# A block of a streaming encoder: the gated product of up pair 19 and the sums over it are issued one weight chunk later

## The chip, the cores and the metric

The kernel runs on one core of one Trainium2 chip. The metric is the time of one execution on the device, in microseconds (us). The kernel before takes 693.18 us (median of 3 runs, 693.14 to 693.18).

The core has a matrix engine (PE, with its weight loads shown apart as PEld), a vector engine (DVE), a scalar engine (ACT), a general engine (POOL) and one that only starts transfers (SP). Each works through its own instructions in the order in which they were issued, and waits for the others through semaphores.

## The reference

One residual layer over x of 512 positions by 1024 channels, in float32:

```
h = rms_norm(x)
proj = h @ w_in                      # 1024 -> conv B, C, in | q, k, v | forget logits | gates
y_conv = (cb * conv3(cc * cin)) @ w_out_conv
y_attn = forgetting_attention(q, k, v, log_f) @ w_out_attn
x = x + (g_conv * y_conv + g_attn * y_attn) @ w_o
h = rms_norm(x)
up = causal_dwconv(h @ w_up, conv_ffn_w)      # 1024 -> 2 * 2816, then 3 taps over the positions
a, b = split(up)
x = x + (silu(a) * b) @ w_down                # 2816 -> 1024
return rms_norm(x)
```

The change lies in the last part: the product with w_up, the taps, silu(a) * b, and the preparation of that product for w_down.

## The kernel before

**Float32 out of two parts.** Every product is made of three passes of the matrix engine, over a high and a low part of each operand. A chunk of weights (128 partitions by 1024 columns for w_up) is loaded into a `raw` tile by SP, `split` lets ACT copy it into the high part (`wh_...`, L275) and DVE subtract that from it to get the low part (`wl_...`, L279). There are two buffers for each of the two parts, so the parts of a chunk can be written once the matrix engine is through with the chunk two places ahead. The chunks come in one fixed stream: for the channel mixer `up0`, `up1`, ... `up43`, with some places taken by chunks `P` and `F` (below).

**The channel mixer.** The 2816 hidden channels are 22 blocks of 128. Pair j is the block j of a and the block j of b, thus the chunks up(2j) and up(2j+1). A pair's product goes through `up`: 8 blocks of 128 rows times 3 passes times 2 halves of 256 positions are 48 matmuls into one PSUM bank for each chunk. `block` puts the passes of the first two row blocks in another order: 8 matmuls with the high part of the weights, 4 with the low part (L327), and then 36 in the plain order (L309). The result is scaled into `fz` (L1170, DVE), goes through the three taps into `fu` (one ACT instruction, L566, and two of DVE, L567 and L570), and `glu` takes silu of a (ACT, L1231) and multiplies by b.

Pairs are taken two at a time (number q = j // 2): the even pair's product is `ge{q}` (POOL, L1234), the odd one's `go{q}` (L1241, on POOL for pairs 17 and 19). From both come sums (`t13`, `t24`: L1251 to L1256, DVE) that serve a product with seven instead of eight block products, and the high and low parts of those sums: `gh` (ACT, L1260) and `gl` (DVE, L1261), which are called the forms here. The forms of one q are four instructions on ACT and four on DVE. The matrix engine reads them only in the phase that follows (`dn`, the product with w_down, with the chunks P and F). The tile of `go{q}` and its sums has one buffer, so go9 may be written only when the forms of go8 are made.

There are two such phases. Phase 0 has pairs 0 to 11, phase 1 has pairs 12 to 21. Pairs 14 and 17 (`SUP[1]`) also take the way with seven products; their results are put together by `merge`, which fills a list with work tagged `e`.

**What sets the order.** Work that isn't urgent is put on a list `later`, as (chunk number from which it is due, a price, tags, function). `split` ends with `run_later`, which takes from the front of the list what is due, as far as a budget of 1.7 us for a chunk reaches, and issues it with the condition that it comes behind the high and the low part of the chunk just split (`after_split`). `flush_only` issues all of a tag at once, also behind the chunk split last. Ahead of the product of q, `glu` flushes all forms of the earlier q.

**POOL and the transfers.** The weights F are sums of weights, made in DRAM while the kernel runs: SP copies (L208), POOL issues additions by transfer (L211, `f34` to `f41` for phase 1), in six steps that `slot()` issues one after the other, once for each chunk. These instructions stand in POOL's row between the products.

The functions below hold the changed lines and what calls them. (go8 belongs to pairs 16 and 17, go9 to pairs 18 and 19; the chunk behind which `sums` comes is up40, the first of pair 20.)

Of the kernel before, what the change touches and what calls it, by code (L numbers as in the profile page):

```python
# [8 lines left out]
F32 = mybir.dt.float32  # L9
F32R = mybir.dt.float32r  # L10
AF = mybir.ActivationFunctionType
ALU = mybir.AluOpType

P = 128
# [4 lines left out]
H = 8  # L19
# [3 lines left out]
NP = FFN // P  # L23
# [19 lines left out]
PHASES = ((0, 12), (12, NP))  # L43
NG = 42
NF = 7
# [15 lines left out]
SUP = ((1, 2, 5), (14, 17))  # L61
# [9 lines left out]
def block_kernel(ctx, tc, xT, vecs, wv, win, wmix, wo, wup, wst, wdp, outT):  # L71
# [3 lines left out]
    nc = tc.nc  # L75
# [6 lines left out]
    def keep(ins):  # L82
        return tc.keep_in_program_order(ins)
# [25 lines left out]
    tbl = cp.tile([4 * H, 1], F32, tag="tbl", name="tbl")  # L109
# [17 lines left out]
    n = 0  # L127
# [28 lines left out]
    later = []  # L156
    held = dict.fromkeys(NRAW, 0)

    def after_split():

        st = ExitStack()
        for ins in order.values():
            st.enter_context(tc.issue_after(ins))
        return st
# [53 lines left out]
    def slot():  # L218

        while todo_bg and todo_bg[0][0] <= make_forms.slot:  # L220
            todo_bg.pop(0)[1]()
        make_forms.slot += 1
# [24 lines left out]
    def flush_only(tags):  # L247

        while n := [n for n, w in enumerate(later) if set(w[2]) & set(tags)]:
            with after_split():  # L250
                later.pop(n[0])[3]()
# [84 lines left out]
    eps = ex[:, NT : NT + 1]  # L336
# [52 lines left out]
    at = ExitStack()  # L389
# [62 lines left out]
    for kb in range(KB):  # L452
        x = xs[kb]
# [12 lines left out]
        for cs in cuts:  # L466
            keep(nc.vector.scalar_tensor_tensor(
                xgl[:, kb, cs], x[:, cs], col(G1 + kb), xgh.bitcast(F32)[:, kb, cs],
                op0=ALU.mult, op1=ALU.subtract,
# [94 lines left out]
    def taps(u, z, w):  # L564

        nc.scalar.activation(u, z, AF.Copy, scale=col(w + 2))  # L566
        nc.vector.scalar_tensor_tensor(  # L567
            u[:, 1:], z[:, : S - 1], col(w + 1), u[:, 1:], op0=ALU.mult, op1=ALU.add
        )
        nc.vector.scalar_tensor_tensor(  # L570
            u[:, 2:], z[:, : S - 2], col(w), u[:, 2:], op0=ALU.mult, op1=ALU.add
        )
# [111 lines left out]
    for t in range(NT):  # L684
        src = pa[t][:, 4 * HD : VW].unsqueeze(1).to_broadcast([P, 4, H])
        nc.vector.tensor_scalar_mul(zn[:, t], src, rc1[:, t : t + 1])

    n = 4 * H
    bf, me, mo = vec[:n, BF : BF + 1], vec[:n, ME : ME + 1], vec[:n, MO : MO + 1]
    z, e, o = (ap.tile([n, S], F32, tag="pp", name=nm, bufs=NPP) for nm in ("fz", "fe", "fo"))  # L690
# [69 lines left out]
    def x_sums(qs):  # L760
        b11, b12, b21, b22 = (xq[:, qs, i, :] for i in range(4))

        def f():
            nc.vector.tensor_sub(b11, b11, b12)
            nc.vector.tensor_sub(b12, b22, b12)

        def g():
            nc.vector.scalar_tensor_tensor(b22, b11, -1.0, b22, op0=ALU.mult, op1=ALU.subtract)
            nc.vector.scalar_tensor_tensor(b21, b22, -1.0, b21, op0=ALU.mult, op1=ALU.subtract)

        return f, g

    k = len(parts) + 2
    for q in (0, 2):
        f, g = x_sums(slice(q, q + 2))
# [8 lines left out]
    for idx in late:  # L784
        kind, i = divmod(idx, 4)
# [7 lines left out]
    n = len(units)  # L793
    make_forms(0, len(GATES), "gate")
    for i in range(n + LA):
# [8 lines left out]
        if 0 <= i - LA < n:  # L804
            pr, e, qb = units[i - LA]
# [5 lines left out]
    halves_of = "p (h c) -> p h c"  # L811
# [6 lines left out]
    def split_next():  # L818
        if len(parts) == chunk.n and stream[chunk.n][0] not in ("dp1", "dp2"):
            split()  # L820
# [85 lines left out]
    k = [c[0] for c in stream].index("mix0")  # L906
# [52 lines left out]
    for j in range(KB):  # L959
        gs = []  # L960
# [25 lines left out]
        a, b = gs  # L986
# [13 lines left out]
    gh = gx.tile([P, NG, 2 * P], F32R, tag="gh", name="gh")  # L1000
    gl = gx.tile([P, NG, 2 * P], F32R, tag="gl", name="gl")
# [36 lines left out]
    def block(name, xh, xl, lead=False):  # L1038
        wh, wl = chunk(name)
        q = acc(f"p_{name}")  # L1040
        for kb in range(KB):
            ks = slice(kb * P, (kb + 1) * P)
            if lead and kb < 2:
                if kb:
                    passes([
                        (q[:, cs], 0, wh[:, b], wl[:, b], xh[:, a, cs], xl[:, a, cs], True, False)
                        for a, b in enumerate((slice(0, P), ks)) for cs in halves
                    ], 4)
                continue
            mm3(q, wh[:, ks], wl[:, ks], xh[:, kb, :], xl[:, kb, :], kb == 0, kb == KB - 1)  # L1050
        return q
# [39 lines left out]
    def up_form(ph, q, g):  # L1091
        if g < 3:
            kb, hs = (2 * q, 2 * q + 1, 2 * q + 1)[g], th[(0, 0, 1)[g]]
            return x1h[:, kb, hs], x1l[:, kb, hs]
        n = XF[ph] + 4 * q + (0, 3, 1, 2)[g - 3]
        return gh[:, n, :], gl[:, n, :]
# [4 lines left out]
    for j in range(KB):  # L1101
        slot()
        if j == 0:
# [6 lines left out]
            op0=ALU.mult, op1=ALU.subtract,  # L1110
# [7 lines left out]
    fp = ctx.enter_context(tc.tile_pool(name="fp", bufs=1))  # L1118
# [22 lines left out]
    def up(j, ph, rb2, pu=None):  # L1141
        uu = []

        def tap(i, z):
            u = fp.tile([P, S], F32, tag="fu", name=f"fu{j}{i}", bufs=3)
            taps(u, z, CF + 3 * (2 * j + i))
            uu.append(u)

        if j in SUP[ph]:
            c = 2 * SUP[ph].index(j)  # L1150
            slot()
            seven(
                UPD[ph][c : c + 2], NU[ph] + c, {j: USETS[j]}, lambda q, g: up_form(ph, q, g), of="x",
                done=lambda i, banks, ids: merge(ph, j, banks, ids, rb2, tap, uu),
            )
            slot()
            return
        evacs = []
        for i in range(2):
            slot()  # L1160
            p = pu[i] if pu else block(f"up{2 * j + i}", x1h, x1l, True)
            if i and j + 1 == PHASES[ph][1]:
                split_next()
                split()
                flush_only((("e",),))
            z = [None]

            def mul(i=i, p=p, z=z):
                z[0] = fp.tile([P, S], F32, tag="fz", name=f"fz{j}{i}", bufs=4)
                nc.vector.tensor_mul(z[0], p, rb2)  # L1170

            evac = [(0.7, mul), (1.4, lambda i=i, z=z: tap(i, z[0]))]
            if i:
                evac.append((0, lambda: glu(ph, j, uu)))
            if any(("e",) in w[2] for w in later):
                later.extend((0, us, (("e",), acc.last) if x == 0 else (("e",),), f) for x, (us, f) in enumerate(evac))
            else:
                for _, f in evac:
                    f()
# [46 lines left out]
    def glu(ph, j, uu):  # L1226
        a, b = uu
        q, k = j // 2, len(parts) - 1
        g0 = place(ph, q)
        with tc.issue_after(order["hi"]) if j + 1 == PHASES[ph][1] else ExitStack():  # L1230
            nc.scalar.activation(a, a, AF.Silu)  # L1231
        if j % 2 == 0:
            ge = glu.even = fp.tile([P, 2, 2 * P], F32, tag="ge", name=f"ge{q}", bufs=2)
            keep(nc.gpsimd.tensor_mul(ge, a.rearrange(halves_of, h=2), b.rearrange(halves_of, h=2)))  # L1234
            return
        flush_only([("q", x) for x in range(q)])
        ge = glu.even
        go = fp.tile([P, 6, 2 * P], F32, tag="gr", name=f"go{q}")

        def mul(eng):  # L1240
            return eng.tensor_mul(go[:, 0:2, :], a.rearrange(halves_of, h=2), b.rearrange(halves_of, h=2))  # L1241

        if j + 1 < PHASES[ph][1]:
            keep(mul(nc.vector if ph and j + 1 in SUP[ph] else nc.gpsimd))
        else:
            later.append((k + 3, 0.7, (("q", q),), lambda: mul(nc.vector)))
        b11, b12 = ge[:, 0, :], ge[:, 1, :]
        b21, b22, t1, t2, t3, t4 = (go[:, i, :] for i in range(6))

        def t13():  # L1250
            nc.vector.tensor_sub(t1, b11, b12)  # L1251
            nc.vector.tensor_sub(t3, b22, b12)

        def t24():
            nc.vector.scalar_tensor_tensor(t2, t1, -1.0, b22, op0=ALU.mult, op1=ALU.subtract)
            nc.vector.scalar_tensor_tensor(t4, t2, -1.0, b21, op0=ALU.mult, op1=ALU.subtract)  # L1256

        def hl(src, gs):
            def f():
                nc.scalar.activation(gh[:, gs, :], src, AF.Copy)  # L1260
                nc.vector.tensor_sub(gl[:, gs, :], src, gh.bitcast(F32)[:, gs, :])  # L1261

            return f


        d = (2, 3, 4) if j + 1 < PHASES[ph][1] else (4, 5, 6)
        w = [(d[0], 0.85, t13), (d[0], 0.85, t24), (d[1], 0.7, hl(ge[:, : 1 + ph, :], slice(g0, g0 + 1 + NF * ph, NF)))]
        w += [(d[x > 0 and 2 or 1], 0.7, hl(go[:, x : x + 2, :], slice(g0 + 1 + x, g0 + 3 + x))) for x in (0, 4, 2)]
        at = next((x for x, i in enumerate(later) if ("e",) in i[2]), len(later))
        later[at:at] = [(k + n, us, (("q", q),), f) for n, us, f in w]  # L1270
        if j == NP - 1:
            src = gh.bitcast(F32)[: 4 * H, g0 + 1, :1]
            later.append((k + 10, 0, (), lambda: nc.scalar.activation(tbl, src, AF.Sqrt, scale=0.0, bias=eps[: 4 * H])))

    def combine(ph, i, banks, ids):

# [261 lines left out]
```

## Time and profile before

| | |
|---|---|
| median of 3 runs | 693.18 us |
| the profiled execution | 693.12 us |
| its span, first to last instruction | 691.3 us |
| outside the span | 1.8 us |
| PE busy | 681.8 us (99%) |
| DVE busy | 555.2 us (80%) |
| ACT busy | 367.9 us (53%) |
| POOL busy | 192.7 us (28%) |
| mean granted clock of the matrix engine | 0.997 |

All times in the profile count from the span's start. A row of the timeline gives the start, the length, the engine, the line of the code, the operation with what it writes and reads, and how often it comes; in brackets stands how long the engine was idle ahead of it, and what ended that. The length of an instruction of DVE or ACT holds a little overlap with the next one (a `gl` of 512 columns is shown as 0.69 us and the next starts 0.60 us behind it); the chain of waits shows the distances without that overlap.

### The profile page before, as it was taken

What the parts mean: (1) busy time and instruction counts of PE and PEld (TensorE: products, weight loads), DVE (VectorE), ACT (ScalarE), POOL (GpSimd) and SP (SyncE); (2) the same over time, 40 slices, a digit from 0 to 9 for tenths busy, and PEclk for the clock granted to TensorE, in tenths of its full rate; (3) what the DMA queues carried; (4) which work ended last, traced back from release to release, by engine and by line L of the source; (5) the groups of instructions that cost most, each with busy time, mean ns of one, the idle gap of its engine ahead of it and who ended that gap; (6) DMA issues with size and microseconds to landing.
All of it is one profiled execution on the core that took longest, in us unless ns stands there. A gap on an engine that the chain in (4) does not pass through costs nothing.

```text
span 691.3 us, 14713 instructions
## 1 busy us (share of the span) xinstructions
PE 681.8 (99%) x5936; PEld 679.9 (98%) x5936; DVE 555.2 (80%) x861; ACT 367.9 (53%) x581; POOL 192.7 (28%) x203
## 2 busy tenths in 40 slices
PE   8999999999999999999999999999999999999996
PEld 8999999999999999999999999999999999999995
DVE  5777887967578778868879699998787898988894
ACT  5675755555555444446564455546444545445672
POOL 6124947542020201214400144340100314332000
PEclk9999999999999999999999999999999999999998
DMA  8628999562577686788997498888945986876513
GB/s 291 240 62 287 217 246 208 129 134 92 167 162 210 166 261 198 239 310 210 161 315 230 129 251 216 184 233 253 250 148 187 288 256 162 191 167 161 192 31 123
DMA packets 66165, 137.54 MB, mean 199 GB/s; under 512 B 5888, under 2 KB 31760, under 8 KB 65840
## 3 DMA queue, kind: packets, MB, share of 16 engines
q1 hardware_dynamic: 45384, 107.28, 46.9%
q0 software_dynamic: 18896, 26.03, 24.4%
q10 hardware_dynamic: 1816, 3.29, 1.3%
q8 instruction: 46, 0.75, 0.4%
q14 instruction: 23, 0.19, 0.1%
HBM read 132.31 MB, written 47.71 MB: 260 GB/s over the span
## 4 chain that ended last, share of the span: by engine, by line
PE 94%; DVE 3%; DMA 1%; ACT 0%; issue 0%; SPq 0%; DVEq 0%; ACTq 0%
PE dn L327 28%; PE p_up L309 18%; PE p_in L309 14%; PE p_wo L309 6%; PE p_up L327 5%; PE yc L309 3%; PE ya L309 3%; PE p_q L309 2%; PE p_k L309 2%; PE o L658 2%; PE pa L477 2%; PE pb L479 1%; PE tp L641 1%; PE pdB L309 1%; PE pdA L309 1%; DVE wl_up L279 1%
## 5 line engine op out<-in xcount | busy, mean ns | idle before, releaser
L211 POOL DMA_DIRECT2D f<-in_wst_dram x69 | 80.0, 1367 | 26.7 <-DMA f<-f 26.3
L309 PE MATMUL p_up<-x1h,wh_up 128*128 128x256 f32 x416 | 81.1, 276 | 0.0
L309 PE MATMUL p_up<-x1h,wl_up 128*128 128x256 f32 x416 | 81.0, 276 | 0.0
L309 PE MATMUL p_up<-x1l,wh_up 128*128 128x256 f32 x416 | 81.0, 276 | 0.0
L279 DVE TENSOR_TENSOR wl_F<-raw_F,wh_F 128x1024 fp32r<-128x1024 f32 (+1 forms) x43 | 56.1, 1304 | 19.0 <-ACT wh_F L275 18.9
L275 ACT ACTIVATE wh_F<-raw_F 128x1024 fp32r<-128x1024 f32 (+1 forms) x43 | 44.5, 1035 | 40.8 <-PE dn L327 26.4
L309 PEld LDWEIGHTS p_up<-x1h,wh_up 128*128 128x128 f32 x416 | 62.7, 188 | 0.0
L309 PEld LDWEIGHTS p_up<-x1l,wh_up 128*128 128x128 f32 x416 | 62.6, 188 | 0.0
L309 PEld LDWEIGHTS p_up<-x1h,wl_up 128*128 128x128 f32 x416 | 62.6, 188 | 0.0
L1234 POOL TENSOR_TENSOR ge<-fu,fu 128x512 f32<-128x512 f32 x11 | 23.2, 2108 | 123.3 <-DVE fu L570 92.6
L309 PE MATMUL p_in<-xgh,wh_in 128*128 128x256 f32 x288 | 56.8, 279 | 0.0
L309 PE MATMUL p_in<-xgh,wl_in 128*128 128x256 f32 x288 | 56.6, 278 | 0.0
L309 PE MATMUL p_in<-xgl,wh_in 128*128 128x256 f32 x288 | 56.5, 278 | 0.0
L275 ACT ACTIVATE wh_P<-raw_P 128x768 fp32r<-128x768 f32 (+1 forms) x43 | 35.2, 820 | 34.5 <-PE dn L327 23.1
L279 DVE TENSOR_TENSOR wl_P<-raw_P,wh_P 128x768 fp32r<-128x768 f32 (+1 forms) x43 | 41.7, 970 | 14.6 <-ACT wh_P L275 8.6
L279 DVE TENSOR_TENSOR wl_up<-raw_up,wh_up 128x1024 fp32r<-128x1024 f32 x34 | 45.2, 1328 | 7.5 <-ACT wh_up L275 7.4
L327 PE MATMUL dn<-gh,wh_F 128*128 128x256 f32 x216 | 51.0, 276 | 0.0
L327 PE MATMUL dn<-gl,wh_F 128*128 128x256 f32 x216 | 51.0, 276 | 0.0
L275 ACT ACTIVATE wh_up<-raw_up 128x1024 fp32r<-128x1024 f32 x34 | 35.8, 1054 | 20.4 <-PE p_up L309 9.8
L309 PEld LDWEIGHTS p_in<-xgh,wh_in 128*128 128x128 f32 x288 | 44.7, 188 | 0.7
L309 PEld LDWEIGHTS p_in<-xgl,wh_in 128*128 128x128 f32 x288 | 43.7, 188 | 0.0
L309 PEld LDWEIGHTS p_in<-xgh,wl_in 128*128 128x128 f32 x288 | 43.6, 188 | 0.0
(343 smaller groups left out, 2208.5 us busy)
## 6 DMA issues: line engine op xcount, KB each, us to landing
raw_F<-f SPq DMA_DIRECT2D x40, 512.0 KB, 5.8
raw_up<-in_wup_dram SPq DMA_DIRECT2D x34, 512.0 KB, 5.6
raw_P<-in_wst_dram SPq DMA_DIRECT2D x40, 384.0 KB, 5.9
raw_in<-in_win_dram SPq DMA_DIRECT2D x24, 512.0 KB, 4.1
f<-in_wst_dram POOLq DMA_DIRECT2D x41, 256.0 KB, 7.7
f<-in_wst_dram SPq DMA_DIRECT2D x19, 512.0 KB, 7.1
f<-in_wst_dram POOLq DMA_DIRECT2D x19, 512.0 KB, 8.4
f<-f SPq DMA_DIRECT2D x38, 256.0 KB, 6.0
```

The source lines that it names most:

```text
L211: return lambda: keep(nc.gpsimd.dma_start(dst, src, accum_op=ALU.add))
L275: ins = nc.scalar.activation(hi, raw, AF.Copy)
L279: ins = nc.vector.tensor_sub(lo, raw, hi.bitcast(F32))
L309: keep(nc.tensor.matmul(out[:, cs], w, x[:, cs], start=start and i == 0 and c == 0, stop=stop and i == 2 and c == len(cut) - 1,))
L327: keep(nc.tensor.matmul(out, wl if x == 1 else wh, xl if x == 2 else xh, start=opens and bk not in seen, stop=closes and bk not in left,))
L477: keep(nc.tensor.matmul(pa[t][:, :VW], xt, w[:, VB:], start=start, stop=stop))
L479: keep(nc.tensor.matmul(pb[t], xt, w[:, :VB], start=start and t % 2 == 0, stop=stop and t % 2 == 1))
L641: keep(nc.tensor.transpose(tp[:, ks], pt[:, ks], ident))
L658: keep(nc.tensor.matmul(o[:, 2 * P * e + c0 : 2 * P * (e + 1)], w, x[:, kb, c0:], start=e == 0 and kb == 0 and i == 0, stop=e == 1 and kb ...
L1234: keep(nc.gpsimd.tensor_mul(ge, a.rearrange(halves_of, h=2), b.rearrange(halves_of, h=2)))
```

## The change

All of `glu` from the flush to the listing of the new forms becomes a function `sums`. For nearly all pairs it is called at once, as before. For an odd pair that comes two places behind one of `SUP[1]` (pair 19 alone) it is put at the front of `later`, due at the next chunk, with price 0.

```diff
-        flush_only([("q", x) for x in range(q)])
         ge = glu.even
-        go = fp.tile([P, 6, 2 * P], F32, tag="gr", name=f"go{q}")
...
+        def sums():
+            flush_only([("q", x) for x in range(q)])
+            go = fp.tile([P, 6, 2 * P], F32, tag="gr", name=f"go{q}")
...
+            if j + 1 < PHASES[ph][1]:
+                keep(mul(nc.vector if ph and j + 1 in SUP[ph] else nc.gpsimd))
...
+            w = [(d[0], 0.85, t13), (d[0], 0.85, t24), (d[1], 0.7, hl(ge[:, : 1 + ph, :], slice(g0, g0 + 1 + NF * ph, NF)))]
+            w += [(d[x > 0 and 2 or 1], 0.7, hl(go[:, x : x + 2, :], slice(g0 + 1 + x, g0 + 3 + x))) for x in (0, 4, 2)]
+            at = next((x for x, i in enumerate(later) if ("e",) in i[2]), len(later))
+            later[at:at] = [(k + n, us, (("q", q),), f) for n, us, f in w]
...
+        if ph and j - 2 in SUP[ph]:
+            later.insert(0, (k + 1, 0, (("q", q),), sums))
         else:
...
+            sums()
```

The numbers at which the new forms of q = 9 are due are the same as before, since k is that of the call of `glu`. What moves is the flush of the forms of q = 8, which was held behind the parts of up39 and is now held behind those of up40, and the product go9.

On DVE, between the low parts of up39 and up41, stands before (`fz190` and `fu190` are the first block of pair 19; names end in a number of the buffer):

```order
L1255 SCALAR_TENSOR_TENSOR go8_7797<-go8_7797 128x256
L1261 TENSOR_TENSOR gl_3989<-ge8_7585,gh_3988 128x2x256
L1256 SCALAR_TENSOR_TENSOR go8_7797<-go8_7797 128x256
L1261 TENSOR_TENSOR gl_3989<-go8_7797,gh_3988 128x512
L1170 TENSOR_TENSOR fz190_7920<-p_up38_7871,rb_n2_4668 128x512
L1261 TENSOR_TENSOR gl_3989<-go8_7797,gh_3988 128x512 x2
L567 SCALAR_TENSOR_TENSOR fu190_7922<-fz190_7920,vec_64,fu190_7922 128x511
L279 TENSOR_TENSOR wl_up40_8009<-raw_up40_7781,wh_up40_8008 128x1024
L570 SCALAR_TENSOR_TENSOR fu190_7922<-fz190_7920,vec_64,fu190_7922 128x510
L1170 TENSOR_TENSOR fz191_7987<-p_up39_7938,rb_n2_4668 128x512
L279 TENSOR_TENSOR wl_up41_8074<-raw_up41_7852,wh_up41_8073 128x1024
```

and in the changed kernel, at the same place of DVE:

```order
L1257 SCALAR_TENSOR_TENSOR go8_7797<-go8_7797 128x256
L1258 SCALAR_TENSOR_TENSOR go8_7797<-go8_7797 128x256
L1171 TENSOR_TENSOR fz190_7920<-p_up38_7871,rb_n2_4668 128x512
L279 TENSOR_TENSOR wl_up40_7999<-raw_up40_7781,wh_up40_7998 128x1024
L567 SCALAR_TENSOR_TENSOR fu190_7922<-fz190_7920,vec_64,fu190_7922 128x511
L1263 TENSOR_TENSOR gl_3989<-ge8_7585,gh_3988 128x2x256
L570 SCALAR_TENSOR_TENSOR fu190_7922<-fz190_7920,vec_64,fu190_7922 128x510
L1263 TENSOR_TENSOR gl_3989<-go8_7797,gh_3988 128x512 x3
L1171 TENSOR_TENSOR fz191_7987<-p_up39_7938,rb_n2_4668 128x512
L279 TENSOR_TENSOR wl_up41_8074<-raw_up41_7852,wh_up41_8073 128x1024
```

The low part of up40 had four forms and one tap instruction between the sums of go8 and itself; now only `fz190` is there, and the four forms stand between it and the low part of up41.

On ACT, from the tap of the chunk up37 to the high part of up41, stands before:

```order
L566 ACTIVATE fu181_7864<-fz181_7862,vec_64 128x512
L1260 ACTIVATE gh_3988<-ge8_7585 128x2x256
L1260 ACTIVATE gh_3988<-go8_7797 128x512 x3
L275 ACTIVATE wh_up40_8008<-raw_up40_7781 128x1024
L566 ACTIVATE fu190_7922<-fz190_7920,vec_64 128x512
L1231 ACTIVATE fu190_7922<-fu190_7922 128x512
L275 ACTIVATE wh_up41_8073<-raw_up41_7852 128x1024
```

and in the changed kernel:

```order
L566 ACTIVATE fu181_7864<-fz181_7862,vec_64 128x512
L275 ACTIVATE wh_up40_7998<-raw_up40_7781 128x1024
L566 ACTIVATE fu190_7922<-fz190_7920,vec_64 128x512
L1262 ACTIVATE gh_3988<-ge8_7585 128x2x256
L1262 ACTIVATE gh_3988<-go8_7797 128x512 x3
L1232 ACTIVATE fu190_7922<-fu190_7922 128x512
L275 ACTIVATE wh_up41_8073<-raw_up41_7852 128x1024
```

The four high parts of the forms have moved behind the high part of up40 and a tap.

On POOL, the end of its row stood so before:

```order
L1234 TENSOR_TENSOR ge9_7869<-fu180_7858,fu181_7864 128x512
L211 DMA f34_6912<-in_wst_dram 256x1x256
L1241 TENSOR_TENSOR go9_8002<-fu190_7922,fu191_7989 128x512
L211 DMA f36_6913<-in_wst_dram 128x256
L211 DMA f37_6914<-in_wst_dram 256x1x128
```

and stands so in the changed kernel:

```order
L1235 TENSOR_TENSOR ge9_7869<-fu180_7858,fu181_7864 128x512
L211 DMA f34_6912<-in_wst_dram 256x1x256
L211 DMA f36_6913<-in_wst_dram 128x256
L1244 TENSOR_TENSOR go9_8010<-fu190_7922,fu191_7989 128x512
L211 DMA f37_6914<-in_wst_dram 256x1x128
```

One addition by transfer, that of f36, now stands ahead of the product go9. The order on PE and on SP is the same as before, and so is that on the other engines at all other places.

More of the change, by code (lines that the diff above doesn't have):

```diff
@@ L1235, in glu @@
             return
-        flush_only([("q", x) for x in range(q)])
         ge = glu.even
-        go = fp.tile([P, 6, 2 * P], F32, tag="gr", name=f"go{q}")
[L1240 to L1244, printed above, removed]
-        else:
-            later.append((k + 3, 0.7, (("q", q),), lambda: mul(nc.vector)))
-        b11, b12 = ge[:, 0, :], ge[:, 1, :]
@@ L1248, in glu @@
[L1248 to L1263, printed above, removed]
@@ L1266, in glu, with mul, t13, t24 @@
[L1266 to L1273, printed above, removed]
+        def sums():
+            flush_only([("q", x) for x in range(q)])
+            go = fp.tile([P, 6, 2 * P], F32, tag="gr", name=f"go{q}")
+            def mul(eng):
+                return eng.tensor_mul(go[:, 0:2, :], a.rearrange(halves_of, h=2), b.rearrange(halves_of, h=2))
+            if j + 1 < PHASES[ph][1]:
+                keep(mul(nc.vector if ph and j + 1 in SUP[ph] else nc.gpsimd))
+            else:
+                later.append((k + 3, 0.7, (("q", q),), lambda: mul(nc.vector)))
+            b11, b12 = ge[:, 0, :], ge[:, 1, :]
+            b21, b22, t1, t2, t3, t4 = (go[:, i, :] for i in range(6))
+            def t13():
+                nc.vector.tensor_sub(t1, b11, b12)
+                nc.vector.tensor_sub(t3, b22, b12)
+            def t24():
+                nc.vector.scalar_tensor_tensor(t2, t1, -1.0, b22, op0=ALU.mult, op1=ALU.subtract)
+                nc.vector.scalar_tensor_tensor(t4, t2, -1.0, b21, op0=ALU.mult, op1=ALU.subtract)
+            def hl(src, gs):
+                def f():
+                    nc.scalar.activation(gh[:, gs, :], src, AF.Copy)
+                    nc.vector.tensor_sub(gl[:, gs, :], src, gh.bitcast(F32)[:, gs, :])
+                return f
+            d = (2, 3, 4) if j + 1 < PHASES[ph][1] else (4, 5, 6)
+            w = [(d[0], 0.85, t13), (d[0], 0.85, t24), (d[1], 0.7, hl(ge[:, : 1 + ph, :], slice(g0, g0 + 1 + NF * ph, NF)))]
+            w += [(d[x > 0 and 2 or 1], 0.7, hl(go[:, x : x + 2, :], slice(g0 + 1 + x, g0 + 3 + x))) for x in (0, 4, 2)]
+            at = next((x for x, i in enumerate(later) if ("e",) in i[2]), len(later))
+            later[at:at] = [(k + n, us, (("q", q),), f) for n, us, f in w]
+            if j == NP - 1:
+                src = gh.bitcast(F32)[: 4 * H, g0 + 1, :1]
+                later.append((k + 10, 0, (), lambda: nc.scalar.activation(tbl, src, AF.Sqrt, scale=0.0, bias=eps[: 4 * H])))
```

## The prediction

> **What bounds the kernel now.** I read the page's first lines, then who waits on the matrix engine, then the chain of waits.
>
> ```profile
> span 691.3 us, 14713 instructions
> PE 681.8 (99%) x5936; PEld 679.9 (98%) x5936; DVE 555.2 (80%) x861; ACT 367.9 (53%) x581; POOL 192.7 (28%) x203
> ```
>
> The matrix engine is the bound nearly everywhere, so a change of order on the other engines is worth what it takes from, or adds to, the gaps of PE. The list of waits of PE has three entries:
>
> ```profile
> PE warm L115 <- DVE ones L107: 1.1, 1, 1.1
> PE pa L477 <- DVE wh_v L273: 0.8, 1, 0.8
> PE p_up L327 <- DVE wl_up L279: 0.7, 1, 0.7
> ```
>
> Two belong to the start of the kernel. The third comes once, for a low part of an up chunk. The timeline of PE shows where, and the view of stretches, cut at the starts of the blocks of up38 to up42, shows what it costs:
>
> ```profile
> 608.87 0.28 PE L327 MATMUL p_up<-x1l,wh_up 128*128 128x256 f32 x1
> 609.88 0.74 PE L327 MATMUL p_up<-x1h,wl_up 128*128 128x256 f32 x4 [0.73 <-DVE wl_up L279]
> ...
> 597.20:602.64 5.44, 5.44 (x51) 5.44 (x49) 4.30 (x7) 3.24 (x5) 0.19 (x1) 1.00 0.84 189
> 602.64:608.08 5.44, 5.44 (x51) 5.44 (x49) 5.44 (x11) 2.83 (x4) 4.24 (x2) 1.00 0.48 151
> 608.08:614.55 6.47, 5.74 (x51) 5.54 (x50) 5.36 (x8) 2.20 (x3) 0.00 (x0) 1.00 0.76 142
> 614.55:619.99 5.44, 5.44 (x51) 5.44 (x50) 3.93 (x7) 2.64 (x4) 3.15 (x3) 1.00 0.89 250
> ```
>
> A block of 48 matmuls takes 5.44 us, 0.113 us for one. That of up40 takes 6.47. The column of DVE is full (5.44 of 5.44) in the block ahead of it. The chain of waits there runs through DVE:
>
> ```profile
> 603.83 0.34 DVE go L1255
> 604.17 0.60 DVE gl L1261
> 604.77 0.34 DVE go L1256
> 605.11 0.60 DVE gl L1261
> 605.71 0.60 DVE fz L1170
> 606.31 1.71 DVE gl L1261 x2
> 608.02 0.66 DVE fu L567
> 608.69 1.15 DVE wl_up L279
> 609.83 0.04 issue
> 609.88 0.74 PE p_up L327 x4
> ```
>
> The low part of up40 is ready at 609.84. The eight matmuls with the high part start at 608.08, the last at 608.87, so PE wants the low part at 608.98 (608.87 + 0.11), 0.90 after the block's start. The four forms (`gl`) ahead of it take 0.60 + 0.60 + 1.71 = 2.91 us.
>
> **The change, part by part.** *The stall.* PE loses 609.88 - 608.98 = 0.90, and the first four matmuls behind the gap take longer than those of a block without one; by the stretches the whole is 6.47 - 5.44 = 1.03 us. That is the term of the sum, if the low part comes by 608.9. Lower and upper ends from other views: the list of waits says 0.73, and the chain leaves PE for 609.88 - 608.69 = 1.19.
>
> *The high part of up40 on ACT.* It stood behind the four `gh`:
>
> ```profile
> 600.49 0.71 ACT L566 ACTIVATE fu<-fz,vec 128x512 f32<-128x512 f32 x1
> 605.14 0.63 ACT L1260 ACTIVATE gh<-go 128x512 fp32r<-128x512 f32 x1 [0.30 <-DVE go L1256]
> 605.68 1.05 ACT L275 ACTIVATE wh_up<-raw_up 128x1024 fp32r<-128x1024 f32 x1
> 614.75 1.06 ACT L275 ACTIVATE wh_up<-raw_up 128x1024 fp32r<-128x1024 f32 x1 [1.97 <-PE p_up L309]
> ```
>
> Now it follows the tap that ends at 601.2, and is held by its buffer: PE must be through with up38, at 602.64. The last row shows how fast that is passed on: PE began up41 at 614.55, and ACT took the buffer of up40 at 614.75, 0.20 later. So it runs from 602.84 to 603.9, in time for DVE. Its data must be there by then:
>
> ```profile
> 591.28 0.54 SPq L182 DMA_DIRECT2D raw_up<-in_wup_dram  x1
> raw_up<-in_wup_dram SPq DMA_DIRECT2D x34, 512.0 KB, 5.6
> ```
>
> Issued at 591.28, with a median of 5.6 us to landing, they are there at 596.9.
>
> *The low part of up40 on DVE.* The sums end 0.34 + 0.34 after 603.83, at 604.51; `fz190` takes 0.60, to 605.11; then the low part. Its price has two rows, the nearest before and one with a product on POOL beside it:
>
> ```profile
> 595.40 2.06 DVE L279 TENSOR_TENSOR wl_up<-raw_up,wh_up 128x1024 fp32r<-128x1024 f32 x1
> 612.19 1.22 DVE L279 TENSOR_TENSOR wl_up<-raw_up,wh_up 128x1024 fp32r<-128x1024 f32 x1 [1.11 <-ACT wh_up L275]
> 595.08 1.30 POOL L1241 TENSOR_TENSOR go<-fu,fu 128x512 f32<-128x512 f32 x1 [4.18 <-ACT fu L1231]
> 603.64 3.23 POOL L1234 TENSOR_TENSOR ge<-fu,fu 128x512 f32<-128x512 f32 x1 [6.25 <-DVE fu L570]
> 606.83 1.06 POOL L211 DMA_DIRECT2D f<-in_wst_dram  x1
> ```
>
> The long one started while POOL's product go8 ran (595.08 to 596.38). Before, ge9 ends at 606.87; a product takes 1.30 alone, so it worked from about 605.6, when `fz190` started, and the `gl` pair behind that took 1.71 instead of 1.20. In the new order `fz190` starts at 604.51, so I expect ge9 to work from then to 605.8, and the low part of up40 to meet it. I take the long price less its overlap, 2.06 - 0.08 = 1.98: ready at 607.1. With the short one, 1.15 by the chain, it is 606.3. Either way it is ahead of 608.98, by 1.9 or 2.7 us, and the gap closes whole.
>
> The Trainium skill, page "SBUF — State Buffer", section "Who interferes with whom", says that a DVE instruction with two SBUF inputs and a GpSimd instruction that reads SBUF exclude each other, and that the one that starts first keeps the shared port to its end. By that rule the low part (two SBUF inputs) waits for ge9's end at 605.8 and is ready at 606.95; the sum is the same, and the margin 2.0 instead of 2.7, which is what the chance of a gap that stays in part rests on. It speaks against the change in so far as a form stood in this place before, and the urgent low part stands there now. The trace agrees in the two lengths of 1.22 and 2.06.
>
> *What comes behind, the forms first.* They cost nothing if the low part of up41 is still in time. From 607.1 DVE does the tap 0.66, a form 0.60, the tap 0.66, three forms 1.80, `fz191` 0.60 and the low part 1.15: ready at 612.6. PE now begins up41 at 608.08 + 5.44 = 613.52 and wants it at 614.42: margin 1.8. Before it was 614.55 + 0.90 against 612.19 + 1.22, or 2.0. The cover is thus about as thick as it was. On ACT the forms' high parts now follow the tap of `fz190`: 605.11 + 0.71, then four of 0.54 (605.14 to 605.68), to 608.0, a bit ahead of DVE's use; the silu waits for DVE's second tap (609.0), and the high part of up41 ends near 610.6, ahead of its use at 611.4. That `gl` waits for `gh` in between is part of the margin.
>
> *The product go9 and the transfer ahead of it.*
>
> ```profile
> 615.22 1.30 POOL L1241 TENSOR_TENSOR go<-fu,fu 128x512 f32<-128x512 f32 x1 [7.34 <-DVE fu L570]
> 616.47 1.90 POOL L211 DMA_DIRECT2D f<-in_wst_dram  x2
> 616.55 0.42 DVE L1252 TENSOR_TENSOR go<-go,ge 128x256 f32<-128x256 f32 x1 [1.48 <-POOL go L1241]
> 618.30 1.21 DVE L279 TENSOR_TENSOR wl_up<-raw_up,wh_up 128x1024 fp32r<-128x1024 f32 x1
> ```
>
> go9 waits for the taps of pair 19, not for its place in the row. Its tile is free once the last form of go8 is made, near 610.8. In the new order the taps end at 612.6 + 0.66 + 0.33 + 0.66 = 614.2; before, go9 started right behind them at 615.22, so this is about 0.9 earlier. The addition of f36, now ahead of go9, is issued at 606.8 to 607.9, behind that of f34 (1.06 each); POOL is idle there for 7.34 us, so it costs nothing unless its own input is late. DVE waits for go9 as before, 1.4 us, which keeps all that follows in its place: the sums, `fz200`, and the low part of up42, before 618.30 to 619.51 against a demand at 619.99 + 0.90 = 620.89; now 0.9 earlier against a demand 1.03 earlier. The margin of 1.4 stays at 1.3. Behind that the order is as before, and each step is about 1 us earlier.
>
> *Queues.* SP's order is the same. Its next load into a `raw` tile waits for the low part of up40, which comes 2.7 us earlier. The forms of q = 8 are done near 610.8 instead of 608.0, and the matrix engine reads them behind up43: three blocks of 5.44 after 613.52, at 629.8.
>
> *The sum.* 693.12 for the profiled execution, less 1.03, is 692.09; against the median of 693.18 (0.06 above the profiled one) it is 692.15, or 0.15% less. The limit below which I call two times of this kernel the same is 0.2%, 1.39 us: the gain is real in this working, and under it.
>
> **The rivals.**
>
> *The gap goes to the next chunk (in part).* For it speaks that the 2.4 us of forms only move from one low part to the next. Against it: 1.8 us of margin at up41 and 1.3 at up42. A product on POOL that meets a form costs 0.8 (2.06 - 1.22), so two such meetings eat most of it. A new gap of 0.5 us gives 692.65; one as long as the old gives 693.18. That is also the case in which the change does nothing: the low part of up40 would have to be held by something else until 608.9.
>
> *Slower: ACT held by a load.* In the new row ACT meets the high part of up40 ahead of the tap and the forms. If up40's load isn't there, the forms, the tap and all of DVE behind them stand still, where before the forms filled that time. It decides from a landing after about 604.7 (602.84 + 1.9), 13.4 us after its issue; to be slower than 694.57 it must land near 607.2 + 1.4 = 609, 17 us or more after it, three times the median. Then the time is 693.18 - 1.03 + 2.5 = 694.65.
>
> *Faster than the gap.* To reach 691.79 another 0.36 us must go. PE's list of waits has no other entry after the start, and all blocks around have 5.44. It could only come from what the trace doesn't resolve, such as gaps too short for the list: 691.7.
>
> **How the numbers follow.** The forecast (gap gone whole, 691.99 to 692.45 by the three views of its size): 0.74. The gap in part or all at a later chunk, or no effect (692.45 to 693.18 and a little above): 0.10. Slower by over 0.2%: 0.06. Faster by over 0.2%: 0.10. So faster 0.10, same 0.74 + 0.10 = 0.84, slower 0.06. The range takes the likeliest case and half of the partial one, 0.79 in all: from 691.9 (1.19 gone, and 0.1 for what runs differ) to 692.7.
>
> **What would show it.** In the profile of the changed kernel PE's wait for `wl_up` is gone from the list, the block of up40 takes 5.44, and the chain stays on PE from the block of up39 on. The low part of up40 starts near 605.1 and is long (about 2 us), ge9 ends near 605.8, the three `gl` stand at about 609 to 610.8, and the low part of up41 is ready by 612.6. All behind it is 1.0 us earlier, with the span at 690.3. I am wrong if a `wl_up` or a `wh_up` of up41 to up43 shows up in PE's list, or if one of `dn` does.

## The result

The changed kernel takes 692.03 us (median of 19 runs, 691.51 to 692.38); the kernel before 693.15 us beside it (19 runs, 692.62 to 695.13). The ratio is 0.9982, with a 95% interval of 0.9975 to 0.9989: faster by 0.11 to 0.25%, or about 1.1 us. The profiled execution took 692.09 us, its span 690.3.

In the profile after, the list of waits of PE has lost its third entry and one of the start, which stands there in some runs and in others not:

```profile
PE warm L115 <- DVE ones L107: 1.1, 1, 1.1
```

The view of stretches, cut at 602.64 and 608.08 as before and from there every 5.44 us (the rows are the blocks of up39, up40 and up41; in this profile each cut lies 0.07 behind the block's first matmul):

```profile
602.64:608.08 5.44, 5.44 (x50) 5.44 (x50) 5.41 (x9) 2.97 (x5) 3.54 (x3) 1.00 0.67 166
608.08:613.52 5.44, 5.44 (x50) 5.44 (x50) 5.44 (x9) 3.21 (x5) 0.00 (x0) 1.00 0.92 221
613.52:618.96 5.44, 5.44 (x50) 5.44 (x50) 3.93 (x8) 2.31 (x4) 2.28 (x2) 1.00 0.75 200
```

PE is busy for all of each block. The chain of waits stays on PE:

```profile
598.65 4.08 PE p_up L309 x36
602.73 1.36 PE p_up L327 x12
604.09 4.08 PE p_up L309 x36
608.17 1.36 PE p_up L327 x12
609.53 4.08 PE p_up L309 x36
613.61 1.36 PE p_up L327 x12
```

On DVE (the timeline, with the lines of the changed kernel) the low part of up40 now stands ahead of the forms:

```profile
603.68 0.42 DVE L1257 SCALAR_TENSOR_TENSOR go<-go 128x256 f32<-128x256 f32 x1
604.13 1.40 DVE L1258 SCALAR_TENSOR_TENSOR go<-go 128x256 f32<-128x256 f32 x1
605.46 0.68 DVE L1171 TENSOR_TENSOR fz<-p_up,rb_n 128x512 f32<-128x512 f32 x1
606.06 1.21 DVE L279 TENSOR_TENSOR wl_up<-raw_up,wh_up 128x1024 fp32r<-128x1024 f32 x1
607.19 0.74 DVE L567 SCALAR_TENSOR_TENSOR fu<-fz,vec,fu 128x511 f32<-128x511 f32 x1
607.85 0.68 DVE L1263 TENSOR_TENSOR gl<-ge,gh 128x512 fp32r<-128x512 f32 x1
608.45 0.74 DVE L570 SCALAR_TENSOR_TENSOR fu<-fz,vec,fu 128x510 f32<-128x510 f32 x1
609.11 1.88 DVE L1263 TENSOR_TENSOR gl<-go,gh 128x512 fp32r<-128x512 f32 x3
610.92 0.68 DVE L1171 TENSOR_TENSOR fz<-p_up,rb_n 128x512 f32<-128x512 f32 x1
611.52 1.21 DVE L279 TENSOR_TENSOR wl_up<-raw_up,wh_up 128x1024 fp32r<-128x1024 f32 x1
...
617.60 1.21 DVE L279 TENSOR_TENSOR wl_up<-raw_up,wh_up 128x1024 fp32r<-128x1024 f32 x1
```

and PE takes the low part of up40 without a break, 0.90 after the block's first matmul:

```profile
608.01 0.28 PE L327 MATMUL p_up<-x1h,wh_up 128*128 128x256 f32 x1
...
608.91 0.62 PE L327 MATMUL p_up<-x1h,wl_up 128*128 128x256 f32 x4
```

The low part is ready when the next instruction starts, at 607.19, 1.7 us ahead of its use. That of up41 is ready at 612.65 against 614.35 (608.01 + 5.44 + 0.90), and that of up42 at 618.73 against 619.79. On ACT and POOL:

```profile
602.77 1.06 ACT L275 ACTIVATE wh_up<-raw_up 128x1024 fp32r<-128x1024 f32 x1 [1.64 <-PE p_up L309]
...
603.57 1.67 POOL L1235 TENSOR_TENSOR ge<-fu,fu 128x512 f32<-128x512 f32 x1 [6.24 <-DVE fu L570]
605.20 1.91 POOL L211 DMA_DIRECT2D f<-in_wst_dram  x2
614.53 1.29 POOL L1244 TENSOR_TENSOR go<-fu,fu 128x512 f32<-128x512 f32 x1 [7.42 <-DMA raw_F<-f]
```

### The profile page after: what moved, and what is told of

Read it like the earlier page. It is cut to its first block, busy times and chain, and to the rows that moved or that the text cites. A ratio compares the mean times of both kernels' runs of the same rounds, so it can differ in the third digit from the quotient of the medians.

```text
span 690.3 us, 14714 instructions
## 1 busy us (share of the span) xinstructions
PE 682.4 (99%) x5936; PEld 681.1 (99%) x5936; DVE 556.0 (81%) x861; ACT 368.5 (53%) x581; POOL 190.9 (28%) x203
## 4 chain that ended last, share of the span: by engine, by line
PE 99%; DVE 0%; DVEq 0%; issue 0%
PE dn L327 29%; PE p_up L309 21%; PE p_in L309 14%; PE p_up L327 6%; PE p_wo L309 6%; PE yc L309 3%; PE ya L309 3%; PE pa L477 2%; PE pb L479 2%; PE p_q L309 2%; PE p_k L309 2%; PE o L658 2%; PE tp L641 1%; PE pdB L309 1%; PE pdA L309 1%; PE s L612 1%
## 5 line engine op out<-in xcount | busy, mean ns | idle before, releaser
L1235 POOL TENSOR_TENSOR ge<-fu,fu 128x512 f32<-128x512 f32 x11 | 21.6, 1968 | 124.1 <-DVE fu L570 94.0
```

## The experiments

Times of single runs of this kernel lie up to 0.7 us about the median, and a few are 1.6 to 2.6 us longer; part of that arises ahead of the channel mixer, where nothing is changed. A gap of PE is read more finely from one profile, as the distance from the first matmul of a block to that of the next, 5.44 us for a block without a gap. Both are given below; where an experiment has a single run, its time says little beside this spread. Theory A is that of the prediction: the gain is the gap that the low part of up40 made, since the forms stood ahead of it.

### The product alone, a chunk later

The flush stays at its old place, only the product go9 and the listing of its forms are put off. That also leaves f36 ahead of go9 on POOL, as in the changed kernel.

```diff
         if ph and j - 2 in SUP[ph]:
+            early = [w for w in later if set(w[2]) & {("q", x) for x in range(q)}]
+            for w in early[: len(early) - 0]:
+                later.remove(w)
+                with after_split():
+                    w[3]()
             later.insert(0, (k + 1, 0, (("q", q),), sums))
```

> The forms of pair 17 stay where they were (behind the parts of up39); only the product go9 is issued a chunk later, which puts the addition of f36 ahead of it on POOL. Theory A (the gain is the gap that the four forms made ahead of the low part of up40): the gap stays, the block of up40 takes 6.4 to 6.5 us, the time is that of the kernel before, 693.1 us, ratio 1.000. Theory B (the gain comes from the product or from the earlier transfer on POOL): the block takes 5.44 us and the time is near 692.05.

Measured: 693.02 us (10 runs) against 693.14 before, ratio 0.9996 (0.9987 to 1.0005). The stretch of up40's block, cut at the first matmuls of up40 and up41:

```profile
607.44:613.97 6.53, 5.81 (x51) 5.61 (x49) 5.42 (x8) 2.20 (x3) 0.67 (x1) 1.00 0.90 146
```

and the entry of up40 in PE's list of waits:

```profile
PE p_up L327 <- DVE wl_up L279: 0.7, 1, 0.7
```

The gap is there, as long as before: PE begins with the low part 0.89 late (609.23 against 607.44 + 0.90). The block is 0.06 longer than the 6.47 of before, and that lies in the matmuls behind the gap. Neither the product nor the earlier transfer on POOL brings a gain that can be seen: the interval leaves out the 0.9984 that theory B would give. What is left is the place of the forms. The high part of up40, which also comes earlier in the changed kernel, is no rival: before, it was done at 606.73 (605.68 + 1.05), and the low part began only at 608.69, behind the forms and the tap.

### One form of four

The same edit, with `early[: len(early) - 1]` in the loop: the last form alone goes behind the parts of up40, and with it one tap instruction falls behind the low part.

> Three of the four forms of pair 17 stay ahead of the low part of up40; only the last one moves behind it, and one tap instruction with it (0.60 + 0.66 = 1.26 us less ahead of the low part). Theory A: the low part was 0.86 us late (ready at 609.84 against 608.98), so 1.26 is enough: ready at about 608.6, block of up40 5.44 us, 692.1 us, the same gain as with all four. Rival: the gain grows with each form that is moved, so one of four gives about a quarter of 1.03: block near 6.2 us, 692.9 us.

Measured: 691.86 us (10 runs) against 693.14, ratio 0.9979 (0.9970 to 0.9989). In the profile of it (an execution of 694.43 us, which runs 2.3 to 2.4 us behind that of the changed kernel from its first 40 us on) the block of up40 takes 5.44 us:

```profile
609.64 1.21 DVE L279 TENSOR_TENSOR wl_up<-raw_up,wh_up 128x1024 fp32r<-128x1024 f32 x1
...
610.38 0.28 PE L327 MATMUL p_up<-x1h,wh_up 128*128 128x256 f32 x1
...
611.29 0.62 PE L327 MATMUL p_up<-x1h,wl_up 128*128 128x256 f32 x4
```

The low part is ready at 610.77 (609.64 + 1.13), 0.5 ahead of its use. The whole gain is there with one form moved. The rival, a gain that grows with each form, falls: its 692.9 us would be a ratio of 0.9997, outside the interval. What counts is whether the low part is still late; the 1.26 us that were moved here clear the 0.86 by which it was. How little would have been enough was not tried.

### The low part three times

In the changed kernel the low part of up40 is computed three times over, into the same place.

```diff
-        ins = nc.vector.tensor_sub(lo, raw, hi.bitcast(F32))
+        for _ in range(3 if nm == "up40" else 1):
+            ins = nc.vector.tensor_sub(lo, raw, hi.bitcast(F32))
```

> The changed kernel, with the low part of up40 computed three times, with the tap instructions of pair 19 between. In the changed kernel it is ready at 607.2 and wanted at 608.9, a margin of 1.7 us. Two more of 1.13 and two taps of 0.66 come ahead of its last end: 610.8. Theory A with that margin: PE waits 1.9 us, the block of up40 takes 7.3 to 7.6 us, time 694.0 to 694.2; up41 just in time. Rival (the margin is thicker, or PE's demand isn't what the row says): a block under 7 us. If the forms pushed on to the next chunk are late too, the block of up41 takes over 5.5 us.

Measured in a single run: 693.75 us, 0.25 to 0.45 under the forecast. The block of up40 began at 607.59 in this execution, 0.42 earlier than in the profile of the changed kernel, which accounts for that. The forecast of the gap holds: 1.82 us in the list of waits, block of up40 7.56, that of up41 5.44.

The timeline, DVE and PE:

```profile
605.63 1.21 DVE L280 TENSOR_TENSOR wl_up<-raw_up,wh_up 128x1024 fp32r<-128x1024 f32 x1
...
609.22 1.21 DVE L280 TENSOR_TENSOR wl_up<-raw_up,wh_up 128x1024 fp32r<-128x1024 f32 x1
...
610.49 0.74 PE L328 MATMUL p_up<-x1h,wl_up 128*128 128x256 f32 x4 [1.82 <-DVE wl_up L280]
...
614.68 1.22 DVE L280 TENSOR_TENSOR wl_up<-raw_up,wh_up 128x1024 fp32r<-128x1024 f32 x1
...
616.06 0.62 PE L328 MATMUL p_up<-x1h,wl_up 128*128 128x256 f32 x4
```

and the stretches of the blocks of up40 and up41:

```profile
607.59:615.15 7.56, 5.74 (x50) 5.54 (x49) 7.56 (x11) 3.27 (x5) 0.24 (x1) 1.00 0.69 166
615.15:620.59 5.44, 5.44 (x50) 5.44 (x49) 4.85 (x9) 2.83 (x4) 3.24 (x2) 1.00 0.67 190
```

The first of three was ready at 606.76 (605.63 + 1.13), 0.83 ahead of the block's start at 607.59, as in the changed kernel. The third came 3.59 us later, at 610.35, and PE began with it 2.00 later than without a gap (610.49 against 607.59 + 0.90). The difference, 1.6, is the margin, against 1.7 read from the profile; PE takes 0.14 from the end of the low part to the first matmul with it. All four forms went behind `fz191` here, and the low part of up41 still came in time, 0.25 ahead (615.81 against 616.06).

### ge9 on DVE

In the changed kernel the product ge9 goes to DVE.

```diff
-            keep(nc.gpsimd.tensor_mul(ge, a.rearrange(...), b.rearrange(...)))
+            keep((nc.vector if j == 18 else nc.gpsimd).tensor_mul(ge, a.rearrange(...), b.rearrange(...)))
```

> The changed kernel with the product ge9 on DVE instead of POOL. In the changed kernel the last sum of go8 (line 1258) took 1.40 us where 0.42 is usual, while ge9 ran on POOL from 603.6 to 605.2. Theory: POOL's product held it up. Then that sum takes 0.42 here, DVE does 0.60 more for the product, and the low part of up40 is ready about 0.4 earlier, at 606.8; time as the changed kernel, 692.05, since the margin is on a path that PE doesn't wait for. Rival: the sum takes 1.4 us all the same (it waits for its own input).

Measured in a single run: 691.51 us, as short as the shortest of the changed kernel's runs. The last sum of go8 and the low part of up40:

```profile
603.14 0.69 DVE L1235 TENSOR_TENSOR ge<-fu,fu 128x512 f32<-128x512 f32 x1
...
604.19 0.43 DVE L1258 SCALAR_TENSOR_TENSOR go<-go 128x256 f32<-128x256 f32 x1
...
605.14 1.22 DVE L279 TENSOR_TENSOR wl_up<-raw_up,wh_up 128x1024 fp32r<-128x1024 f32 x1
...
607.47 0.28 PE L327 MATMUL p_up<-x1h,wh_up 128*128 128x256 f32 x1
```

The sum takes 0.43 instead of 1.40. The low part is ready at 606.27, 1.20 ahead of the block's start at 607.47, where it was 0.82 ahead in the changed kernel (607.19 to 608.01): 0.38 earlier, as expected. POOL's product was what held up the sum. The blocks of up39 to up41 stay at 5.44, as in the changed kernel, so nothing of it reaches PE. The block of up40 began 0.54 earlier than in that kernel's profile, for reasons ahead of it, and that is all by which the time is under the forecast.

### Pair 11 too, and the changed kernel again

In the profile of the changed kernel PE itself lists no gap behind the start, but the list of waits of its weight loads has one, for the low part of P19:

```profile
PEld dn L327 <- DVE wl_P L279: 0.2, 1, 0.2
```

The same row stands in the list of the kernel before. The gap is in the second step of phase 0, where the last form of go4 and a tap stand ahead of that low part (the changed kernel):

```profile
470.29 0.68 DVE L1263 TENSOR_TENSOR gl<-go,gh 128x512 fp32r<-128x512 f32 x1
470.89 0.74 DVE L570 SCALAR_TENSOR_TENSOR fu<-fz,vec,fu 128x510 f32<-128x510 f32 x1
471.55 0.95 DVE L279 TENSOR_TENSOR wl_P<-raw_P,wh_P 128x768 fp32r<-128x768 f32 x1
```

The edit puts off the flush at pair 11, in the same way:

```diff
-        if ph and j - 2 in SUP[ph]:
+        if j in (11, 19):
             later.insert(0, (k + 1, 0, (("q", q),), sums))
```

> The changed kernel, with the product of pair 11 (the last of phase 0) and its flush issued a chunk later too. In the changed kernel the low part of P19 comes 0.2 us late at 472.5 (it starts at 471.55 behind a form and a tap instruction), and the 18 matmuls there take 2.37 us instead of 2.04. Here the last form of go4 and the second tap come behind that low part, 0.60 + 0.66 = 1.26 us. Theory A (what stands ahead of a late low part costs PE its lateness and a slow start): the stretch from 466.24 on takes 9.52 us for 84 matmuls without a gap, 0.3 us less than the changed kernel, 691.7 us; ratio to the kernel before 0.9978 to 0.998. Rival: the form comes late for the step that uses it, or the gap goes to the next low part (F19): same time as the changed kernel or up to 0.3 us more.

> The changed kernel again, on the same chip and in the same rounds as the run with pair 11 moved too, so that the two can be set side by side: 692.0 us, ratio to the kernel before 0.998 to 0.9985, and PE's small wait for the low part of P19 near 472 in the profile.

Measured, side by side on one chip (before: 693.14 us, 21 runs): with pair 11 too 691.67 us (11 runs), ratio 0.9981 (0.9972 to 0.9990); the changed kernel again 691.78 us (11 runs), ratio 0.9982 (0.9974 to 0.9991). In the profiles, the first matmuls of phase 0's product, then those with the low part of P19, with pair 11 too:

```profile
465.99 0.28 PE L327 MATMUL dn<-gh,wh_P 128*128 128x256 f32 x1
...
472.11 0.84 PE L327 MATMUL dn<-gh,wl_P 128*128 128x256 f32 x6
```

and in the changed kernel again:

```profile
465.94 0.28 PE L327 MATMUL dn<-gh,wh_P 128*128 128x256 f32 x1
...
472.27 0.98 PE L327 MATMUL dn<-gh,wl_P 128*128 128x256 f32 x6
```

The way to that low part takes 6.12 us with pair 11 too and 6.33 in the changed kernel, and the six matmuls that follow 0.84 against 0.98. So the small gap of 0.2 and its slow start of 0.14 are gone in the profile. The timing can't show a third of a microsecond: the two medians differ by 0.11 us, and the intervals of the ratios are 0.0017 to 0.0018 wide. That the version with both is faster than the changed kernel is shown by this stretch of the profile alone; the times show neither a gain nor a loss between the two.

## Why the prediction was right

- *The stall.* The term of 1.03 us was right. The block of up40 went from 6.47 to 5.44, the profiled execution from 693.12 to 692.09, as the sum had it; the medians differ by 1.12. That the profiled executions agree with the sum to 0.01 is luck, since single runs differ by more (the block of up40 began 0.07 earlier in the profile after); what is shown is the 1.03 in the block. The medians of the run with one form and of the changed kernel taken again lie 1.28 and 1.36 under that of before. The three intervals hold 1.03, so whether the rest is more than spread isn't shown. Of the three sizes that the views gave, 0.73, 1.03 and 1.19, that of the stretches is the one that came out. The list of waits showed less since a matmul stands there with 0.28 us, though the next follows 0.11 behind it: it hides 0.17 of each gap (0.90 - 0.17 = 0.73). That the gap was caused by the forms' place, and not by the product or the transfer, is shown by the run with the product alone.
- *The high part of up40.* Forecast 602.84 to 603.9, held by PE's release of the buffer of up38; measured 602.77 to 603.83, with that releaser.
- *The low part of up40.* Forecast ready at 607.1; measured 607.19. But the step is wrong in how it got there, and the sign that I gave for it didn't come: the low part was to start near 605.1 and take about 2 us, with ge9 ending near 605.8; it started at 606.06, and ge9 ended at 605.24. I had ge9 start to work when `fz190` started, and the low part meet it. It was the sum ahead of `fz190` that met it (1.40 instead of 0.42), and the low part took its short time, 1.21. The delay was about 1.0 in place of 0.8, on an instruction two places earlier; since all of these stand in one row on DVE the end is nearly the same. That it agrees to 0.1 is partly luck.
- *The forms and up41.* Forecast: forms until 610.8, low part of up41 ready at 612.6, margin 1.8. Measured: 610.9, 612.65, 1.7. The gap didn't go to the next chunk. The run with the low part thrice shows that the forms can come later still, and up41 is in time.
- *go9 and up42.* The product began at 614.53, forecast 614.2: it came 0.69 earlier than before, not 0.9. The sum left out the 0.23 us between the end of the last tap and the product, which stand in both kernels (614.99 to 615.22 before, 614.30 to 614.53 after). So the low part of up42 came 0.70 earlier (617.60 against 618.30) for a demand 1.10 earlier (619.79 against 620.89), and its margin, counted to its full length as in the forecast, was 0.98 instead of 1.3. The row of the product names a transfer as what it waited for; since the 0.23 behind the tap are the same as before, and the run with pair 11 too names the tap after an equal idle time of 7.42, a cost of the transfer isn't shown. The two additions on POOL took 1.91 from 605.20 on, in idle time.
- *Faster than the gap.* I wrote that PE's list had no other entry behind the start. The gap of 0.2 at P19 was too short for it (0.17 hidden), but the weight loads' list of waits shows it, in the profile before as well, so it could have been read there. With its slow start it is 0.34 us, so it would have made that rival's 0.36 had the change touched it; it didn't.
- *The bound of 0.2%.* The forecast was a gain under what I called the limit. With 19 runs of each, the interval (0.11 to 0.25% less) leaves out no change; the gain is real and of the size forecast.

## What to carry to other kernels

In this kernel the matrix engine is busy 99% of the time, and the change of order on the other engines was worth the lateness of the one operand that it waited for (0.90 us) plus a slow start of 0.13. So measure the block with the gap against one without, and find how far the operand is late. Taking one form or all four from ahead of it gave the same block of 5.44 us, since each clears the lateness, and the next operand's margin was larger than what was pushed onto it. Look for such gaps in the weight loads' list of waits too: the matmuls' list left out the one of 0.2 us here.

## What the runs showed of the hardware

With the new order on DVE a product on POOL got its turn earlier, and a DVE instruction was held up by it. In the changed kernel the sums of go8 on lines 1257 and 1258 stand 0.45 us apart, where an instruction of this size takes 0.34 in the chain of waits of before. ge9 ended at 605.24, and the sum that started at 604.13 took 1.40, until 605.5. In the kernel before, DVE had a form between those two sums; both took 0.42, and ge9 showed 3.23 us, with its end at 606.87, 1.16 behind the 605.71 at which `fz190` stands in the chain. All the profiles agree: with a form between the sums (before, the product alone, one form of four) ge9 showed 3.22 to 3.23 us and the second sum 0.42; without one (the changed kernel in both its profiles, the low part three times, pair 11 too) ge9 showed 1.67 or 1.68 and the sum 1.40. So a shorter list of DVE work can make POOL's product earlier and a DVE instruction longer at once. The run with ge9 on DVE (0.43 for that sum) shows that it is the product.

That ge9 got in during the break of 0.1 us between the two sums is inferred. The break is DVE's own, since the same 0.45 stands between them with ge9 on DVE (603.74 to 604.19), and the end of ge9 less the 1.30 us of a product is 603.94, an estimate that lies near it; no run changed the break alone.

The Trainium skill, page "SBUF — State Buffer", section "SBUF: two separate sides", says that whichever of the two starts first gets the shared port for the whole instruction, and the other blocks. The traces agree on that in the two lengths of the same sum, 1.40 and 0.43. The start that a row of POOL shows is not that moment: ge9 stands at 603.57, ahead of the sum at 603.68, which took its usual 0.42 all the same.
